# Two-layer streaming encoder: the low part of a pair's two direct factors made by a negation on ACT and an accumulating DMA instead of a subtraction on DVE

## The chip, the cores and the metric

One Trainium2 chip, one core. The metric is the device time of one execution in microseconds, on the core that runs the program; the time before is the median of three runs.

## The reference, cut to what matters

One inference step of a two-layer encoder for 512 prompt frames and 8 x 16 sample frames, so 640 rows of 1024 channels. Layer 0 has an S5 and attention mixer, layer 1 a Mamba-2 mixer. Each layer begins and ends with a gated feed-forward, so there are four of them, and the change lies in these alone:

```python
def swiglu(x, w_gate, w_up, w_down):
    return (jax.nn.silu(x @ w_gate) * (x @ w_up)) @ w_down

x = layer_norm(ALPHA * x + 0.5 * swiglu(x, ffn_w_gate[l, 0], ffn_w_up[l, 0], ffn_w_down[l, 0]),
               ln_g[l, 0], ln_b[l, 0])
```

The weights are float32: gate and up are 1024 x 2816, down is 2816 x 1024. In the kernel the 2816 hidden channels are 22 rows of 128.

## The kernel before

**Arithmetic.** Every float32 factor is split into a high part, cast to the fp32r format, and a low part, the rest. A product is three matmuls: high by high, low by high, high by low. `split` (L99) makes both parts: ACT casts the source into the high part (L100), and DVE subtracts this from the source (L101). The weights arrive by DMA from SP in tiles `raw` of 128 x 1024 (512 KB, four buffers), and the parts are put in tiles `w` (L110: two units of high and low, 128 x 2 x 2 x 512, six buffers) and one single unit `w1` (L107, one buffer).

**Feed-forward.** `ffn` (L226) runs four times, named ffn0, ffn1, ffn2 and ffn3. Rows 0 and 1 and the gate of rows 2 and 3 are computed directly. All other rows go in pairs (`pair`, L400), gate first and up after it, and each is one call of `matrix` (L370) that replaces eight block products of a 2 x 2 by 2 x 2 scheme with seven. A product (L362) is 12 matmuls of 320 columns, so a matrix has 84.

**Operands of a matrix.** `operands` (L339) loads two raw tiles, `r0` with the blocks b11 and b21 and `r1` with b12 and b22. Two of the seven factors, b11 and b21 themselves, are split straight from `r0` into tile u; these are the two direct factors. Then four totals (`total`, L347) are formed in place, over the raw blocks, on DVE: b11 becomes b12 - b11, then b12, b22 and b21 in turn. Between them stand the splits of b22 and of the new b11 (tile v), of the new b12 and b22 (tile w) and of the new b21 (tile o, the single unit). The first total therefore overwrites half of `r0`, from which u has been split. The totals are told to be queued behind the low part of b22 on DVE (`state["lo"]`).

**Order of the products.** TensorE runs the factors in the order 1, 5, 6, 2, 7, 3, 4: u, v, w, u, w, v, o. After product 1 ACT copies the result x into z (L383), since product 6 adds to z; products 5 and 6 are copied aside by ACT (L379). The four quarters of the result leave PSUM by `take`: x (quarter 0,0) after product 2, z (quarter 1,1) after product 7, w (quarter 1,0) after product 3, z (quarter 0,1) after product 4, which goes on adding to z and so waits until the take of (1,1) has been done. For the gate the takes are additions on DVE (L408) and SiLU on ACT (L410), for up they are additions and products on DVE (L416, L418, L420).

**Between the matrices.** Rows are gathered by four. The order is up, gate, up and gate of the next four rows, and then `down` of the earlier four rows; so four matrices stand between two downs, and three before the last down of a feed-forward. In ffn1, ffn2 and ffn3 most downs are `down7` (L463), also with seven products; half of its results go to DVE (L511), half to ACT, which scales them into `ev` (L514), and from there by an accumulating DMA on POOL into `yacc` (L515). In ffn0 and ffn3 side work of the mixers is interleaved.

**Order of instructions.** Each engine runs its own queue in order. A scheduler sets these orders when the program is built, from its own estimates of durations and from the dependencies; semaphore waits follow from the dependencies, on buffers too. So a change of an instruction moves others.

Of the kernel before, what the change touches and what calls it, by code (L numbers as in the profile page):

```python
# [10 lines left out]
F32 = mybir.dt.float32  # L11
# [3 lines left out]
ALU = mybir.AluOpType  # L15
# [22 lines left out]
def kernel(ctx: ExitStack, tc: tile.TileContext, I, O, phases=PHASES):  # L38
    nc = tc.nc
# [31 lines left out]
    def bank_a():  # L71
        return bank(next(state["a"]))
# [26 lines left out]
    def split(hi, lo, src):  # L99
        nc.scalar.copy(hi, src)  # L100
        return nc.vector.tensor_tensor(lo, src, hi.bitcast(F32), op=ALU.subtract)  # L101

    def raw_tile():
        return pools["raw"].tile([128, 1024], F32, name="raw")

    def unit():
        return pools["w1"].tile([128, 2, 512], F32R, name="w1")  # L107

    def two_units():
        return pools["w"].tile([128, 2, 2, 512], F32R, name="w")  # L110

    def split2(w, src):

        return split(w[:, :, 0], w[:, :, 1], src.rearrange("p (j c) -> p j c", j=2))
# [111 lines left out]
    def ffn(i, ph, last, side=None):  # L226
# [4 lines left out]
        with ExitStack() as st:  # L231
# [63 lines left out]
            for r in range(2):  # L295
# [3 lines left out]
                for c in range(2):  # L299
                    p = bank_a()[:, :Q] if r else sums[c]  # L300
# [38 lines left out]
            def operands(src0, src1):  # L339
                r0, r1 = raw_tile(), raw_tile()  # L340
                nc.sync.dma_start(r0, src0)
                nc.sync.dma_start(r1, src1)
                b11, b21, b12, b22 = r0[:, :512], r0[:, 512:], r1[:, :512], r1[:, 512:]
                u, v, w = (two_units() for _ in range(3))
                o = unit()

                def total(o, v, w):  # L347
                    with tc.issue_after(state["lo"]):
                        V.tensor_tensor(o, v, w, op=ALU.subtract)  # L349

                split2(u, r0)
                state["lo"] = split(v[:, 1, 0], v[:, 1, 1], b22).ins
                total(b11, b12, b11)
                split(v[:, 0, 0], v[:, 0, 1], b11)
                total(b12, b22, b12)
                total(b22, b22, b11)
                split2(w, r1)
                total(b21, b21, b22)
                split(o[:, 0], o[:, 1], b21)
                return {1: u[:, 0], 2: u[:, 1], 3: v[:, 1], 4: o, 5: v[:, 0], 6: w[:, 1], 7: w[:, 0]}  # L360
# [39 lines left out]
            def pair(f, before=None):  # L400
# [25 lines left out]
                for n, take in (("w_gate", gate), ("w_up", up)):  # L426
                    if n == "w_gate" and f == 2:
                        tick("gate")
                        continue
                    if n == "w_up" and before is not None:  # L430
                        down(before)
                    with ExitStack() as q:
                        if f == 2:
                            for k in ("acc0", "xc"):
                                if k in state:
                                    q.enter_context(tc.issue_after(state[k]))
                        A = operands(I[n][i, f], I[n][i, f + 1])
                    if n == "w_up":
                        for r in range(2):
                            ht[f + r] = h_tile()  # L440
                    matrix(A, take)
                    if n == "w_up" and seven(f):
                        row_sums(f)
                    tick("gate" if n == "w_gate" else "up")
# [1576 lines left out]
```

## Time and profile before

| what | value |
|---|---|
| median of three runs | 2541.68 us (2533.86 to 2542.25) |
| the profiled execution | 2534.06 us |
| its span in the profile | 2532.4 us |
| mean granted TensorE clock | 0.997 |
| loads of `w_gate`, `w_up`, `w_down` by SP | 88 each, 512 KB |
| data moved by DMA | 324.80 MB |

The page lists busy time by engine, the chain of work that ended last, and groups of instructions by line. PE stands for TensorE's matmuls and PEld for its weight loads, DVE for VectorE, ACT for ScalarE, POOL for GpSimd, SP for SyncE, which issues most DMAs. A row of a window shows its length, then the busy time and count of each engine, the clock, the busy share of the DMA engines and GB/s. A row of the timeline shows start and duration of an instruction, or of several of one kind that follow each other (x2).

### The profile page before, as it was taken

Reading aid. Unit: us, or ns where it says so; the run is one execution under the profiler, and the core shown is the slowest. Engines: PE = TensorE matmul, PEld = TensorE weight load, DVE = VectorE, ACT = ScalarE, POOL = GpSimd, SP = SyncE. Lnnn points to the kernel's source line nnn. Section 1 sums busy time; section 2 is a strip of 40 time slices with the busy share of each in tenths; the row PEclk is TensorE's granted clock in tenths of the full one; section 3 lists DMA queues with packets and bytes.
Section 4 is the critical chain, followed back from the end, with each engine's and each line's share of the span. In section 5 each row is a group of like instructions: output and inputs, shape, how many; then the busy total and the mean of one; then the engine's idle time right before and its main releaser. Section 6 shows DMA issues by size and latency. Waiting matters only on the chain. (4 is left out here: it accounts for less than half of the span.)

```text
span 2532.4 us, 40815 instructions
## 1 busy us (share of the span) xinstructions
PE 2488.3 (98%) x15551; PEld 2282.8 (90%) x15551; DVE 2018.3 (80%) x3505; ACT 1272.1 (50%) x2389; POOL 372.9 (15%) x492
## 2 busy tenths in 40 slices
PE   9999999999999999999999999999999999999998
PEld 8999999878779999999999999999999879999997
DVE  7788777666878888878988887777576789998887
ACT  4443444336744555553455554566565543554542
POOL 0000001210130000013000002311121151112121
PEclk9999999999999999999999999999999999999999
DMA  5332335443221433462144434456464722555563
GB/s 186 109 101 87 107 118 155 144 160 109 84 84 59 116 104 98 113 162 68 59 113 112 121 100 131 150 163 196 151 214 135 244 72 94 158 149 164 154 173 115
DMA packets 179253, 324.80 MB, mean 128 GB/s; under 512 B 21312, under 2 KB 92608, under 8 KB 178544
## 3 DMA queue, kind: packets, MB, share of 16 engines
q1 hardware_dynamic: 165200, 293.83, 36.7%
q0 software_dynamic: 13856, 28.35, 5.7%
q8 instruction: 122, 2.00, 0.3%
q14 instruction: 75, 0.61, 0.1%
HBM read 259.56 MB, written 40.54 MB: 119 GB/s over the span
## 5 line engine op out<-in xcount | busy, mean ns | idle before, releaser
L101 DVE TENSOR_TENSOR w<-raw,w 128x512 fp32r<-128x512 f32 (+2 forms) x721 | 626.4, 890 | 84.0 <-ACT w L100 81.2
L100 ACT CAST w<-raw 128x512 fp32r<-128x512 f32 (+1 forms) x721 | 531.5, 769 | 317.2 <-DVE raw L349 153.2
L366 PE MATMUL bank<-xhi,w 128*128 128x320 f32 x2432 | 540.4, 310 | 2.9 <-DVE s L408 1.9
L146 PE MATMUL bank<-xhi,w 128*128 128x256 f32 (+2 forms) x2272 | 497.6, 311 | 6.7 <-DVE hf L288 1.7
L366 PE MATMUL bank<-T,w 128*128 128x320 f32 x2736 | 428.4, 309 | 3.6 <-ACT bank L383 1.7
L366 PEld LDWEIGHTS bank<-xhi,w 128*128 128x128 f32 x2432 | 406.8, 188 | 8.7 <-DVE s L408 3.1
L366 PEld LDWEIGHTS bank<-T,w 128*128 128x128 f32 x2736 | 407.0, 188 | 6.6 <-ACT bank L383 3.9
L146 PEld LDWEIGHTS bank<-xhi,w 128*128 128x128 f32 x2272 | 376.9, 187 | 16.3 <-issue 3.9
L366 PE MATMUL bank<-xlo,w 128*128 128x320 f32 x1216 | 375.2, 309 | 0.0
L146 PE MATMUL bank<-xlo,w 128*128 128x256 f32 (+2 forms) x1136 | 350.5, 309 | 2.0 <-DVE xlo L211 1.8
L146 PE MATMUL bank<-w,h 128*128 128x512 f32 x1488 | 346.5, 391 | 0.0
L146 PEld LDWEIGHTS bank<-w,h 128*128 128x128 f32 x1488 | 277.1, 188 | 57.5 <-ACT h L100 1.4
L366 PEld LDWEIGHTS bank<-xlo,w 128*128 128x128 f32 x1216 | 228.2, 188 | 0.0
L146 PEld LDWEIGHTS bank<-xlo,w 128*128 128x128 f32 x1136 | 213.6, 188 | 3.3 <-DVE xlo L211 2.1
L349 DVE TENSOR_TENSOR raw<-raw 128x512 f32<-128x512 f32 x304 | 211.5, 696 | 3.4
L515 POOL DMA_DIRECT2D yacc<-ev x84 | 72.6, 888 | 689.4 <-ACT ev L514 610.8
L502 PE MATMUL bank<-w,h 128*128 128x512 f32 x576 | 134.5, 389 | 0.0
L502 PEld LDWEIGHTS bank<-w,h 128*128 128x128 f32 x576 | 108.1, 188 | 22.4
L379 ACT COPY mx<-bank 128x320 f32<-128x320 f32 x152 | 64.6, 425 | 104.4 <-PE bank L366 104.1
L511 DVE SCALAR_TENSOR_TENSOR yacc<-bank,yacc 128x512 f32<-128x512 f32 x84 | 57.8, 688 | 72.0 <-PE bank L502 71.9
L223 DVE SCALAR_TENSOR_TENSOR yacc<-bank,yacc 128x512 f32<-128x512 f32 x120 | 81.8, 686 | 34.1 <-PE bank L146 33.4
L514 ACT ACTIVATE ev<-bank 128x512 f32<-128x512 f32 x84 | 50.2, 597 | 116.2 <-PE bank L502 112.9
(437 smaller groups left out, 3427.6 us busy)
## 6 DMA issues: line engine op xcount, KB each, us to landing
raw<-in_w_gate_dram SPq DMA_DIRECT2D x88, 512.0 KB, 3.6
raw<-in_w_up_dram SPq DMA_DIRECT2D x88, 512.0 KB, 4.1
raw<-in_w_down_dram SPq DMA_DIRECT2D x88, 512.0 KB, 3.6
raw<-in_m_in_dram SPq DMA_DIRECT2D x52, 512.0 KB, 4.4
yacc<-ev POOLq DMA_DIRECT2D x84, 256.0 KB, 4.7
raw<-in_m_out_dram SPq DMA_DIRECT2D x24, 512.0 KB, 4.5
csb<-cs_d SPq DMA_DIRECT2D x20, 512.0 KB, 5.3
h<-in_ssd_h_dram SPq DMA_DIRECT2D x16, 512.0 KB, 6.1
```

What stands on the lines that cost most here:

```text
L100: nc.scalar.copy(hi, src)
L101: return nc.vector.tensor_tensor(lo, src, hi.bitcast(F32), op=ALU.subtract)
L146: state["pe"] = nc.tensor.matmul(ps, a, b, start=(k == 0), stop=(k == n - 1)).ins
L223: state["acc"] = nc.vector.scalar_tensor_tensor(ya, pb, scale, ya, op0=ALU.mult, op1=ALU.add).ins
L349: V.tensor_tensor(o, v, w, op=ALU.subtract)
L366: nc.tensor.matmul(ps, A[p][:, a, k * 128:k * 128 + 128], X[p][b][:, k, :], start=(first and n == 0), stop=(n == 11), skip_group_check=True)
L379: nc.scalar.copy(e[n], ps)
L502: nc.tensor.matmul(ps, a[:, u], b[:, v], start=(first and n == 0), stop=(n == 5), skip_group_check=True)
L511: V.scalar_tensor_tensor(ya, ps, 0.5 / ALPHA, ya, op0=ALU.mult, op1=ALU.add)
L514: nc.scalar.mul(e, ps, 0.5 / ALPHA)
L515: nc.gpsimd.dma_start(yacc[:, t, 512 * j:512 * j + 512], e, accum_op=ALU.add)
```

## The change

In `operands` the one call `split2(u, r0)` is replaced. ACT still casts `r0` into the high parts of u. ACT then multiplies these by -1 into the low parts of u, and POOL issues a DMA that adds `r0` to them; so the low part is again `r0` minus its high part. DVE no longer subtracts there. The DMA reads `r0`, so the first total, which overwrites half of `r0`, has to wait until it has landed; the matmuls with u's low parts wait for it too.

```diff
@@ operands @@
-                split2(u, r0)
+                nc.scalar.copy(u[:, :, 0], r0.rearrange("p (j c) -> p j c", j=2))
+                nc.scalar.mul(u[:, :, 1], u[:, :, 0].bitcast(F32), -1.0)
+                nc.gpsimd.dma_start(u[:, :, 1].bitcast(F32), r0.rearrange("p (j c) -> p j c", j=2),
+                                    accum_op=ALU.add)
                 state["lo"] = split(v[:, 1, 0], v[:, 1, 1], b22).ins
                 total(b11, b12, b11)
```

`operands` is called 76 times. Three lines are added, so later lines of the changed kernel are three higher (L383 is L386 there). The scheduler moves other instructions with it. Three places show how, all from ffn1: the up matrix of rows 6 and 7, whose operands are made while the down of rows 2 to 5 runs, and the gate matrix of rows 8 and 9 after it.

DVE, operands of the up matrix, before; raw_8744 and raw_8745 are `r0` and `r1`, w_8748, w_8749, w_8750 and w1_8751 are u, v, w and o, and w_8887 is u of the gate matrix after it:

```order
L101 TENSOR_TENSOR w_8748<-raw_8744,w_8748 128x2x512 [waits DMAHW2_49,Activation_49]
L101 TENSOR_TENSOR w_8749<-raw_8745,w_8749 128x512 [waits DMAHW3_49,Activation_49]
L349 TENSOR_TENSOR raw_8744<-raw_8745,raw_8744 128x512 [waits DVE_49]
L511 SCALAR_TENSOR_TENSOR yacc_84<-bank_8629,yacc_84 128x512 [waits PE_49]
L349 TENSOR_TENSOR raw_8745<-raw_8745 128x512 [waits DVE_49]
L101 TENSOR_TENSOR w_8749<-raw_8744,w_8749 128x512 [waits Activation_49]
L349 TENSOR_TENSOR raw_8745<-raw_8745,raw_8744 128x512 [waits DVE_49]
L511 SCALAR_TENSOR_TENSOR yacc_84<-bank_8627,yacc_84 128x512 [waits PE_49]
L349 TENSOR_TENSOR raw_8744<-raw_8744,raw_8745 128x512 [waits DVE_49]
L101 TENSOR_TENSOR w_8750<-raw_8745,w_8750 128x2x512 [waits Activation_49]
L101 TENSOR_TENSOR w_8887<-raw_8883,w_8887 128x2x512 [waits DMAHW4_49,Activation_49]
```

DVE, the same place in the changed kernel; raw_8767 and raw_8768 are `r0` and `r1`, w_8772, w_8773 and w1_8774 are v, w and o:

```order
L514 SCALAR_TENSOR_TENSOR yacc_84<-bank_8650,yacc_84 128x512 [waits PE_49]
L101 TENSOR_TENSOR w_8772<-raw_8768,w_8772 128x512 [waits DMAHW3_49,Activation_49]
L514 SCALAR_TENSOR_TENSOR yacc_84<-bank_8652,yacc_84 128x512 [waits DVE_49,PE_49]
L349 TENSOR_TENSOR raw_8767<-raw_8768,raw_8767 128x512 [waits DMAHW2_49,DMASW0_49]
L514 SCALAR_TENSOR_TENSOR yacc_84<-bank_8650,yacc_84 128x512 [waits PE_49]
L349 TENSOR_TENSOR raw_8768<-raw_8768 128x512 [waits DVE_49]
L101 TENSOR_TENSOR w_8772<-raw_8767,w_8772 128x512 [waits Activation_49]
L349 TENSOR_TENSOR raw_8768<-raw_8768,raw_8767 128x512 [waits DVE_49]
L514 SCALAR_TENSOR_TENSOR yacc_84<-bank_8650,yacc_84 128x512 [waits PE_49]
L349 TENSOR_TENSOR raw_8767<-raw_8767,raw_8768 128x512 [waits DVE_49]
L101 TENSOR_TENSOR w_8773<-raw_8768,w_8773 128x2x512 [waits Activation_49]
L101 TENSOR_TENSOR w1_8774<-raw_8767,w1_8774 128x512 [waits Activation_49]
```

Both low parts of u (w_8748 and w_8887) have gone, and the first total of raw_8767 now waits for a DMA of POOL's queue (DMASW), with two results of the down (L511, now L514) and the other totals behind it.

ACT, from v's second high part to the first copies of the up matrix, before; w_8887, w_8888 are u and v of the gate matrix, and L383 is the copy of x into z:

```order
L100 CAST w_8749<-raw_8744 128x512 [waits DVE_49]
L514 ACTIVATE ev_8718<-bank_8626 128x512 [waits DMASW7_49,PE_49,Activation_49]
L100 CAST w_8750<-raw_8745 128x2x512 [waits DVE_49]
L100 CAST w_8887<-raw_8883 128x2x512 [waits DMAHW4_49]
L514 ACTIVATE ev_8734<-bank_8626 128x512 [waits DMASW0_49,PE_49,Activation_49]
L100 CAST w1_8751<-raw_8744 128x512 [waits DVE_49]
L100 CAST w_8888<-raw_8884 128x512 [waits DMAHW5_49,PE_49]
L383 COPY bank_7735<-bank_8768 128x320 [waits PE_49]
L100 CAST w_8888<-raw_8883 128x512 [waits DVE_49]
```

ACT, the same place in the changed kernel; w_8911 and w_8912 are u and v of the gate matrix, L386 is the copy into z and L352 the negation:

```order
L100 CAST w_8772<-raw_8767 128x512 [waits DVE_49]
L517 ACTIVATE ev_8757<-bank_8649 128x512 [waits DMASW7_49,PE_49]
L100 CAST w_8773<-raw_8768 128x2x512 [waits DVE_49]
L351 CAST w_8911<-raw_8907 128x2x512 [waits DMAHW4_49]
L100 CAST w1_8774<-raw_8767 128x512 [waits DVE_49]
L386 COPY bank_7754<-bank_8792 128x320 [waits PE_49]
L352 ACTIVATE w_8911<-w_8911 128x2x512 [waits Activation_49]
L382 COPY mx_8819<-bank_8793 128x320 [waits PE_49]
L100 CAST w_8912<-raw_8908 128x512 [waits DMAHW5_49]
L382 COPY mx_8833<-bank_7754 128x320 [waits PE_49]
L100 CAST w_8912<-raw_8907 128x512 [waits DVE_49]
```

The negation for the gate matrix now stands behind the copy into z of the up matrix, which waits for PE, and so the DMA that follows it is issued later than that; v's first high part moves behind that copy and the next one as well.

DVE, operands of the gate matrix and the first takes of the up matrix (L416, L418), before; raw_8883 and raw_8884 are the gate's `r0` and `r1`:

```order
L349 TENSOR_TENSOR raw_8883<-raw_8884,raw_8883 128x512 [waits DVE_49]
L349 TENSOR_TENSOR raw_8884<-raw_8884 128x512 [waits DVE_49]
L101 TENSOR_TENSOR w_8888<-raw_8883,w_8888 128x512 [waits Activation_49]
L349 TENSOR_TENSOR raw_8884<-raw_8884,raw_8883 128x512 [waits DVE_49]
L349 TENSOR_TENSOR raw_8883<-raw_8883,raw_8884 128x512 [waits DVE_49]
L101 TENSOR_TENSOR w_8889<-raw_8884,w_8889 128x2x512 [waits Activation_49]
L416 TENSOR_TENSOR hf_8823<-bank_8768,s_8514 128x320 [waits PE_49]
L101 TENSOR_TENSOR w_9008<-raw_9004,w_9008 128x2x512 [waits DMAHW6_49,Activation_49]
L418 TENSOR_TENSOR hf_8837<-bank_7735,mx_8795 128x320 [waits PE_49]
```

DVE, the same place in the changed kernel, where the takes are L419 and L421 and the gate's tiles raw_8907 and raw_8908:

```order
L101 TENSOR_TENSOR w_8912<-raw_8908,w_8912 128x512 [waits DMAHW5_49,Activation_49]
L419 TENSOR_TENSOR hf_8847<-bank_8792,s_8537 128x320 [waits PE_49]
L349 TENSOR_TENSOR raw_8907<-raw_8908,raw_8907 128x512 [waits DMAHW4_49,DMASW4_49]
L349 TENSOR_TENSOR raw_8908<-raw_8908 128x512 [waits DVE_49]
L421 TENSOR_TENSOR hf_8861<-bank_7754,mx_8819 128x320 [waits PE_49]
L101 TENSOR_TENSOR w_8912<-raw_8907,w_8912 128x512 [waits Activation_49]
L349 TENSOR_TENSOR raw_8908<-raw_8908,raw_8907 128x512 [waits DVE_49]
L421 TENSOR_TENSOR hf_8861<-bank_8793,mx_8833 128x320 [waits PE_49]
```

Before, all four totals and w's low part stood ahead of the take of (0,0). Now the first total, with its wait for the DMA, stands between that take and the take of (1,1), and w's low part has moved behind all takes of the up matrix.

## Prediction before the run

> **What bounds the kernel now.** I read the page's busy times first, then the end of the chain, a table of windows over one stretch of the feed-forward, and the timeline of that stretch.
>
> ```profile
> span 2532.4 us, 40815 instructions
> PE 2488.3 (98%) x15551; PEld 2282.8 (90%) x15551; DVE 2018.3 (80%) x3505; ACT 1272.1 (50%) x2389; POOL 372.9 (15%) x492
> ```
>
> ```profile
> 2501.66 0.47 PE bank L1491 x2
> ```
>
> PE is idle for 2532.4 - 2488.3 = 44.1 us, and the chain leaves PE at 2502.1, so 30.3 of these are the tail of the last layer norm. Only some 14 us are left between the matmuls. No edit off PE can win more.
>
> The second feed-forward (ffn1), from the end of its first seven-product down, stage by stage (four matrices, then the next down):
>
> ```profile
> core 0: us, PE busy (x) PEld busy (x) DVE busy (x) ACT busy (x) POOL busy (x), PEclk, DMA share, GB/s
> 881.40:893.70 12.30, 12.30 (x85) 12.27 (x84) 11.50 (x18) 6.10 (x11) 0.85 (x1) 1.00 0.63 166
> 893.70:906.00 12.30, 12.30 (x86) 12.30 (x85) 11.84 (x22) 7.87 (x16) 0.00 (x0) 1.00 0.28 88
> 906.00:918.30 12.30, 12.30 (x86) 12.30 (x85) 8.61 (x12) 6.84 (x10) 0.00 (x0) 1.00 0.26 85
> 918.30:930.60 12.30, 12.30 (x86) 12.30 (x85) 12.03 (x22) 6.92 (x14) 0.00 (x0) 1.00 0.15 44
> 930.60:955.00 24.40, 24.40 (x110) 20.23 (x109) 17.16 (x24) 11.92 (x17) 5.14 (x6) 1.00 0.62 139
> ```
>
> PE never stops, at full clock, and a matrix lasts 12.3 us. DVE is busy for 11.5 to 12.0 of 12.3 us in three of four: DVE just keeps up, and a DVE that has to wait there soon makes PE wait.
>
> **What is removed and added.** There are 304 totals (L349) at four per call, so `operands` runs 76 times.
>
> ```profile
> L101 DVE TENSOR_TENSOR w<-raw,w 128x1024 fp32r<-128x1024 f32 x248 | 301.4, 1228 | 28.5 <-ACT w L100 27.8
> L100 ACT CAST w<-raw 128x1024 fp32r<-128x1024 f32 x248 | 255.3, 1050 | 137.8 <-DVE raw L349 55.4 <-PE bank L366 26.4 <-PE bank L146 25.4
> L349 DVE TENSOR_TENSOR raw<-raw 128x512 f32<-128x512 f32 x304 | 211.5, 696 | 3.4
> L515 POOL DMA_DIRECT2D yacc<-ev x84 | 72.6, 888 | 689.4 <-ACT ev L514 610.8 <-DMA yacc<-ev 56.1 <-ACT w L100 18.4
> ```
>
> DVE loses 76 x 1.23 = 93 us of work. Since PE is idle in none of these windows, that alone is worth nothing. ACT gets 76 negations; none is in the trace, and I take the cast of the same shape, 1.05 us: 80 us more on an engine that is half idle, free as busy time, but 1.05 us in a chain. POOL gets 76 issues of about 0.9 us, harmless by themselves.
>
> The price is a wait. The first total writes b11 over half of `r0`, which the DMA now reads. Before, it followed the subtraction on DVE's own queue; now it waits until the transfer has landed. Queued behind it on DVE are the other totals, the low parts of v, w and o, and the takes that empty PE's banks; behind the casts that need those totals stand, on ACT, the copy of `r0` for the next matrix and the copies into z that PE needs.
>
> **How long the add takes.** An accumulating DMA of 512 KB is not in the trace. The nearest rows are the 256 KB ones from `ev` to `yacc`: first all 84 from issue to landing, then queue 0 in the window 864 to 886, where it carries seven of them and nothing else, then plain 512 KB loads on the same queue.
>
> ```profile
> DMA to landing us min/median/max: 3.3/4.7/6.6
> ```
>
> ```profile
> q0 software_dynamic: 1004, 1.83, 47.5%
> ```
>
> ```profile
> T<-in_ln_gb_dram POOLq DMA_DIRECT2D x8, 512.0 KB, 5.4
> ```
>
> Seven took 47.5% of 22 us on all engines, so 1.5 us each. Another 256 KB adds 1.5 us: 4.7 + 1.5 = 6.2 us, which I take, being nearest to the row of the same operation and above the plain load. The ends are 3.3 (the shortest, if size cost nothing) and 9.4 (twice the median); 4.8 and 8.1 come from the shortest and longest plus 1.5.
>
> **The walk through one stretch.** Times are from E = 881.43, PE's first matmul after the down. The first rows are DVE and ACT, the last PE.
>
> ```profile
> 872.79 1.57 ACT L100 CAST w<-raw 128x1024 fp32r<-128x1024 f32 x2
> 875.81 0.69 DVE L349 TENSOR_TENSOR raw<-raw 128x512 f32<-128x512 f32 x1
> 878.22 0.69 DVE L349 TENSOR_TENSOR raw<-raw 128x512 f32<-128x512 f32 x1
> 878.94 2.00 ACT L100 CAST w<-raw 128x1024 fp32r<-128x1024 f32 x2 [0.74 <-DVE raw L349]
> ...
> 881.33 1.13 ACT L100 CAST w<-raw 128x512 fp32r<-128x512 f32 x2
> ...
> 883.39 0.41 ACT L383 COPY bank<-bank 128x320 f32<-128x320 f32 x1 [0.93 <-PE bank L366]
> ```
>
> ```profile
> 890.99 0.48 DVE L418 TENSOR_TENSOR hf<-bank,mx 128x320 f32<-128x320 f32 x1
> ```
>
> ```profile
> 881.43 0.46 PE L366 MATMUL bank<-xhi,w 128*128 128x320 f32 x2
> ...
> 893.74 0.45 PE L366 MATMUL bank<-xhi,w 128*128 128x320 f32 x2
> ```
>
> A matrix is 12.31 us, seven products of 1.76. Product 6, third, adds to z and needs the copy into z by 3.5; the last needs the take of (1,1) by 10.55.
>
> *Up of rows 6 and 7.* The copy of `r0` and the high part of b22 end at -7.1, the negation at -6.0, the add lands at +0.2. Before, the first total began at 875.81, -5.6: 5.8 us later now. Two totals, a take, v's low part and another total run to 3.2 at 0.6 each. ACT then casts w (4.3), copies the next `r0` (5.3) and casts o (5.9), and only then copies z (6.3). Before, that copy ended at 2.4, so a cover of 1.1 us is gone and PE waits 6.3 - 3.5 = 2.8.
>
> *The next add.* Its negation now stands behind the z copy: 6.3 to 7.4, landed at 13.6. Two totals run to 14.9 and the take of (1,1) to 15.4; the last product could start at 10.55 + 2.8 = 13.4, so PE waits 2.0 more, and this matrix ends at 17.2. Before, that take began at 890.99, 9.6.
>
> *Gate of rows 8 and 9.* w's low part now stands behind eleven rows of takes, sums and low parts and ends at 23.2; its product needs it at 20.9: 2.3. The next negation ends at 22.4, the add lands at 28.6, three DVE rows and the take run to 30.9, needed at 30.1: 0.8. End 32.7.
>
> *Up of rows 8 and 9.* z copied 0.3 late; negation ends 36.1, add lands 42.3, six DVE rows and the take run to 46.1, needed at 43.6: 2.5. End 47.9, where PE needs 36.9. The fourth matrix holds no add and catches nothing up.
>
> So such a stretch loses 2.8 + 2.0 + 2.3 + 0.8 + 0.3 + 2.5 = 10.7, say 11 us. A check: from one add to the next run the add 6.2, three totals 2.1, cast of w 1.05, copy 1.05, cast of o 0.6 and negation 1.05, 12.1 us without the copies and SiLUs between them (0.4 to 2 us), against 12.3 for PE. The circle is just longer than a matrix. Walked again with 5.0 us the stretch loses 6.2: some 4 us of loss per us of landing.
>
> **The sum.** A feed-forward has five stretches: three like this, 33; the last without its fourth matrix, about 8; the first, where the walk finds three waits of 2.4, 0.2 and 2.8, 5.5. That is 46.5, and 4 x 46.5 = 186 us. I price ffn0 and ffn3 alike, though the side work in them moves rows. On the profiled execution's own time, 2534.06 us: 2720. The median shown, 2541.68, is 7.6 above it: **2728 us**.
>
> **Rivals.**
>
> *The add is hidden, and it is no slower.* If size cost nothing and each add landed like the shortest row, in 3.3 us, the first total would come at -2.7, the z copy in time, and each take before its due. It decides at about 3.8 us: below, the first landing in a stretch still leaves the copies their slack. The gate's late low part alone remains (DVE order, not landing), at most 1 us in four stretches per feed-forward, 16 us, of which DVE's 1.2 us less per matrix gives some back in ffn3, where PE is short by 0.2 to 1.9 us per 50:
>
> ```profile
> 2150.00:2200.00 50.00, 48.10 (x320) 46.72 (x319) 47.72 (x74) 28.02 (x49) 5.21 (x4) 1.00 0.46 150
> ...
> 2350.00:2400.00 50.00, 49.84 (x279) 45.10 (x278) 43.70 (x64) 24.95 (x40) 11.10 (x11) 1.00 0.60 162
> ```
>
> Some +7 remains: 2549, within 0.5%. Against it: only the shortest of 84 is so fast, at half the size. Chance 0.08. The Trainium skill (DMA: Bandwidth & Descriptors, "Anatomy of one DMA") fits a DMA from GpSimd with 2.0 us plus bytes at 436 GB/s, which for 512 KB gives an estimate of 3.2 us and so this case. By that fit the 256 KB rows should take 2.6 us; the trace shows 4.7, so I do not follow it.
>
> *Worse landing.* Each matrix loads 1 MB of weights, and 12.3 us now also carry 3.0 us of add on the same engines; the add's issue stands behind POOL's own waits (L515 idles 689.4 us in all). In ffn3 the DMA share is already 0.46 to 0.60. With 8.1 us a stretch loses 11 + 1.9 x 4 = 18.6, and all of it 186 x 18.6 / 11 = 315: 2857. For it: more traffic than in any window here. Against it: the measured 4.7 already includes neighbours in the same queue. Chance 0.17.
>
> **How the numbers follow.** The forecast, with landings from 4.6 to 7.3, has 0.75. At 7.3 the sum is 186 x 15.4 / 11 = 260, 2802; at 4.6 it is 186 x 4.6 / 11 = 78, 2620. I put the range at 2615 to 2810; left out are the hidden add and most of the worse landing. About 0.5%, 12.7 us, is what a measurement of this kernel can tell from no change. Slower takes the forecast, the worse landing: 0.92; same 0.06; faster 0.02, since 14 us of idle PE is all there is.
>
> **What would show it.** In the changed profile the first total should be DVE's costliest wait, on the add from POOL, some 3 to 6 us each time; the add should take about 6 us to land; PE should be busy for near 2488 us still, but idle some 230, behind ACT's copy into z, DVE's takes and DVE's low part of w; the four windows should read 13 to 17 us instead of 12.3, and the downs still 24. The forecast is wrong if adds land under 4 us, if DVE reaches the first total late anyway, or if PE idles on something else, such as weights that load late.

## The result, and the profile after

The changed kernel takes **2786.28 us** (median of five runs, 2784.65 to 2792.93) against 2541.58 us for the kernel before (also five runs, 2533.86 to 2542.25), a ratio of 1.098 with a 95% interval of 1.096 to 1.100. It is slower, inside the range of 2615 to 2810, and 58 us above the predicted 2728. The profiled execution took 2792.93 us.

The page of the changed kernel:

```profile
span 2791.2 us, 40959 instructions
PE 2573.0 (92%) x15551; PEld 2342.9 (84%) x15551; DVE 1940.7 (70%) x3429; ACT 1338.3 (48%) x2465; POOL 462.3 (17%) x568
```

The span grew by 2791.2 - 2532.4 = 258.8 us. PE's idle time went from 44.1 to 218.2 us, so 174 us of it is waiting. The other 85 us is PE's busy time, 2573.0 against 2488.3, for the same 15551 matmuls. DVE lost 78 us of work and ACT gained 66; neither number is in the span.

**The wait.** From the waits of the changed kernel (engine, tile and line, what released it: us in total, times, longest):

```profile
DVE raw L349 <- DMA w<-raw: 302.6, 69, 7.7
PE bank L369 <- DVE hf L421: 60.6, 27, 4.9
PE bank L369 <- DVE s L411: 52.1, 14, 5.7
PE bank L505 <- DVE yacc L514: 34.2, 12, 6.1
PE bank L369 <- ACT mx L382: 12.4, 9, 2.8
PE bank L369 <- DVE w L101: 3.1, 6, 1.3
```

The first total now waits for the add in 69 of 76 calls, 4.4 us each; before, all 304 totals together had 3.4 us of idle time ahead of them. PE in turn waits for what is queued behind that total on DVE: the takes of the up matrix (hf), of the gate (s), and the results of the down (yacc). The add itself, from issue to landing:

```profile
DMA to landing us min/median/max: 5.0/6.6/9.8
```

**One stretch.** The same stretch as in the prediction (ffn1, behind the first seven-product down), matrix by matrix, in windows of the changed kernel:

```profile
933.75:951.10 17.35, 14.67 (x89) 14.40 (x88) 10.12 (x18) 8.63 (x13) 1.35 (x2) 0.90 0.44 107
951.10:968.30 17.20, 13.48 (x82) 13.02 (x81) 11.09 (x19) 8.43 (x16) 1.20 (x1) 0.90 0.38 92
968.30:985.20 16.90, 14.43 (x88) 14.16 (x87) 9.37 (x14) 7.52 (x12) 1.22 (x1) 0.90 0.48 120
985.20:997.60 12.40, 12.40 (x86) 12.32 (x85) 11.71 (x21) 7.91 (x15) 0.00 (x0) 1.00 0.15 51
```

Three matrices with an add last about 17 us instead of 12.3, the fourth, without one, 12.4. DVE is now busy for 9 to 11 of 17 us: it waits. And the clock, the column behind POOL, has fallen to 0.90 in just these three windows. The timeline shows both causes: ACT's negation (L352), POOL's issue (L353) and DVE's first total (L349), then PE:

```profile
936.46 0.42 ACT L386 COPY bank<-bank 128x320 f32<-128x320 f32 x1
936.82 1.05 ACT L352 ACTIVATE w<-w 128x1024 fp32r<-128x1024 f32 x1
...
938.16 1.20 POOL L353 DMA_DIRECT2D w<-raw  x1 [4.26 <-ACT w L352]
...
945.12 1.42 DVE L349 TENSOR_TENSOR raw<-raw 128x512 f32<-128x512 f32 x2 [3.79 <-DMA w<-raw]
...
962.50 1.42 DVE L349 TENSOR_TENSOR raw<-raw 128x512 f32<-128x512 f32 x2 [5.65 <-DMA w<-raw]
...
977.14 1.42 DVE L349 TENSOR_TENSOR raw<-raw 128x512 f32<-128x512 f32 x2 [5.23 <-DMA w<-raw]
```

```profile
932.25 1.66 PE L505 MATMUL bank<-w,h 128*128 128x512 f32 x6 [1.69 <-DVE yacc L514]
...
942.40 1.92 PE L369 MATMUL bank<-T,w 128*128 128x320 f32 x12
946.99 0.56 PE L369 MATMUL bank<-xhi,w 128*128 128x320 f32 x2 [2.68 <-DVE hf L421]
...
947.56 0.74 PE L369 MATMUL bank<-xhi,w 128*128 128x320 f32 x2
...
951.27 0.46 PE L369 MATMUL bank<-xhi,w 128*128 128x320 f32 x2
...
965.02 0.90 PE L369 MATMUL bank<-xhi,w 128*128 128x320 f32 x2 [3.72 <-DVE s L411]
...
981.40 0.73 PE L369 MATMUL bank<-xhi,w 128*128 128x320 f32 x2 [2.48 <-DVE hf L421]
```

The add issued at 938.16 has landed by 945.1, 7 us later; DVE stands for 3.79 us, PE for 2.68. Behind each such gap a pair of matmuls takes 0.74 us instead of 0.46 for 3 to 4 us. In a window of that time and in one behind it:

```profile
947.50:951.10 3.60, 3.60 (x16) 3.60 (x15) 3.27 (x8) 2.93 (x4) 0.00 (x0) 0.53 0.00 0
951.30:952.10 0.80, 0.80 (x7) 0.80 (x7) 0.80 (x3) 0.70 (x2) 0.00 (x0) 1.00 0.00 0
```

PE is never idle there, and the granted clock is 0.53. The three matrices last 51.45 us, 36.93 at full pace; 8.88 us of the difference are the three gaps, the other 5.6 us are in the slower matmuls behind them.

### The profile page after: what moved, and what is told of

It reads as the page before. It is cut to its first block, busy times and chain, and to the rows that moved or that the text cites. A ratio compares the mean times of both kernels' runs of the same rounds, so it can differ in the third digit from the quotient of the medians.

```text
span 2791.2 us, 40959 instructions
## 1 busy us (share of the span) xinstructions
PE 2573.0 (92%) x15551; PEld 2342.9 (84%) x15551; DVE 1940.7 (70%) x3429; ACT 1338.3 (48%) x2465; POOL 462.3 (17%) x568
## 5 line engine op out<-in xcount | busy, mean ns | idle before, releaser
L100 ACT CAST w<-raw 128x512 fp32r<-128x512 f32 (+1 forms) x645 | 458.4, 735 | 561.3 <-DVE raw L349 438.7
L369 PE MATMUL bank<-xhi,w 128*128 128x320 f32 x2432 | 586.1, 329 | 125.3 <-DVE hf L421 60.6
L101 DVE TENSOR_TENSOR w<-raw,w 128x512 fp32r<-128x512 f32 (+1 forms) x645 | 543.3, 861 | 123.5 <-ACT w L100 121.7
L369 PEld LDWEIGHTS bank<-xhi,w 128*128 128x128 f32 x2432 | 440.0, 204 | 144.7 <-DVE hf L421 68.8
L349 DVE TENSOR_TENSOR raw<-raw 128x512 f32<-128x512 f32 x304 | 210.4, 692 | 305.8 <-DMA w<-raw 302.6
L146 PEld LDWEIGHTS bank<-xhi,w 128*128 128x128 f32 x2272 | 380.3, 189 | 19.7 <-issue 4.9
L369 PE MATMUL bank<-xlo,w 128*128 128x320 f32 x1216 | 394.4, 324 | 0.0
L146 PE MATMUL bank<-w,h 128*128 128x512 f32 x1488 | 348.0, 392 | 1.5 <-ACT h L100 1.5
L369 PEld LDWEIGHTS bank<-xlo,w 128*128 128x128 f32 x1216 | 246.3, 203 | 0.4
L353 POOL DMA_DIRECT2D w<-raw x76 | 94.7, 1247 | 806.9 <-ACT w L352 529.9
L146 PEld LDWEIGHTS bank<-xlo,w 128*128 128x128 f32 x1136 | 215.3, 190 | 3.3 <-DVE xlo L211 2.0
L505 PE MATMUL bank<-w,h 128*128 128x512 f32 x576 | 144.0, 403 | 36.1 <-DVE yacc L514 34.2
L505 PEld LDWEIGHTS bank<-w,h 128*128 128x128 f32 x576 | 109.8, 193 | 64.4 <-DVE yacc L514 38.6
L514 DVE SCALAR_TENSOR_TENSOR yacc<-bank,yacc 128x512 f32<-128x512 f32 x84 | 57.9, 689 | 77.0 <-PE bank L505 76.9
L146 PE MATMUL bank<-w,og 128*128 128x512 f32 x432 | 103.8, 395 | 0.9 <-DVE og L101 0.8
```

The lines of the kernel that those rows point to most:

```text
L146: state["pe"] = nc.tensor.matmul(ps, a, b, start=(k == 0), stop=(k == n - 1)).ins
L353: nc.gpsimd.dma_start(u[:, :, 1].bitcast(F32), r0.rearrange("p (j c) -> p j c", j=2), accum_op=ALU.add)
L369: nc.tensor.matmul(ps, A[p][:, a, k * 128:k * 128 + 128], X[p][b][:, k, :], start=(first and n == 0), stop=(n == 11), skip_group_check=True)
L505: nc.tensor.matmul(ps, a[:, u], b[:, v], start=(first and n == 0), stop=(n == 5), skip_group_check=True)
L514: V.scalar_tensor_tensor(ya, ps, 0.5 / ALPHA, ya, op0=ALU.mult, op1=ALU.add)
```

## The experiments

Three theories. **A**: the price is the first total's wait for the landed add, on the circle copy, negation, add, totals, casts, next copy; the longer matmuls follow from PE's gaps. **B**: the adds' traffic, or POOL's issues, slow the kernel by themselves. **C**: ACT's negation, in front of copies that PE needs, is the cost. Ratios are to the kernel before, run on the same chip beside each.

**1. No total over r0 (e1b).** The adds stay; in three of four feed-forwards nothing waits for them but the matmuls.

```diff
-                total(b11, b12, b11)
-                split(v[:, 0, 0], v[:, 0, 1], b11)
+                t11, t21 = (wk.tile([128, 512], F32, name=n, bufs=1) if ph != "ffn3" else b
+                            for n, b in (("t11", b11), ("t21", b21)))
+                total(t11, b12, b11)
+                split(v[:, 0, 0], v[:, 0, 1], t11)
                 total(b12, b22, b12)
-                total(b22, b22, b11)
+                total(b22, b22, t11)
                 split2(w, r1)
-                total(b21, b21, b22)
-                split(o[:, 0], o[:, 1], b21)
+                total(t21, b21, b22)
+                split(o[:, 0], o[:, 1], t21)
```

> The changed kernel, but in ffn0, ffn1 and ffn2 the totals that would overwrite r0 write into two tiles of their own, so that no total waits for the add; ffn3, where no room is left, stays as changed. All 76 adds and negations remain. Theory A (the cost is the wait of the first total for the landed add, on the circle of copy, negation, add, totals, casts, and the half-rate matmuls that follow PE's gaps): the losses of ffn0 to ffn2 (42 + 64 + 67 us of the 245) go and ffn3's 78 stay: 2615 to 2640 us, PE busy falls by some 55 us from 2573, and the first total's wait on the add is there 19 times instead of 69. Theory B (the traffic of the adds or POOL's issues slow the kernel by themselves): 2740 to 2790. Theory C (ACT's negation, in front of the copies that PE needs, is the cost): 2720 to 2790.

Measured: 2612.41 us, ratio 1.029 (1.027 to 1.030), just under the interval that A gave. POOL's loads of layer-norm rows (L171) mark the phases: the first of T stands at the end of ffn0, the first of h ahead of ffn3, the last of T behind it. Before, changed, and this kernel:

```profile
L171 POOL DMA_DIRECT2D T<-in_ln_gb_dram x8: 538/550/598, 414.6 to 2489.2; - x8
...
L171 POOL DMA_DIRECT2D h<-in_ln_gb_dram x2: 543/602/660, 1992.0 to 1992.7; - x2
```

```profile
L171 POOL DMA_DIRECT2D T<-in_ln_gb_dram x8: 546/570/598, 456.6 to 2748.0; - x8
...
L171 POOL DMA_DIRECT2D h<-in_ln_gb_dram x2: 548/602/655, 2172.9 to 2173.6; - x2
```

```profile
L171 POOL DMA_DIRECT2D T<-in_ln_gb_dram x8: 546/570/598, 412.9 to 2565.4; - x8
...
L171 POOL DMA_DIRECT2D h<-in_ln_gb_dram x2: 551/603/655, 1993.3 to 1994.0; - x2
```

Up to ffn3 this kernel is as fast as the one before (1993.3 against 1992.0; the changed one is at 2172.9), with all its adds and negations. From there to the last load it takes 572.1 us, the changed kernel 575.1, the one before 497.2. So where no total waits, the loss is gone, and where it still waits, in ffn3, nearly all of it has stayed (75 of 78 us).

**2. The first total alone moved (e1).** The fourth total still writes over b21:

```diff
-                total(b11, b12, b11)
-                split(v[:, 0, 0], v[:, 0, 1], b11)
+                t11 = wk.tile([128, 512], F32, name="t11", bufs=1) if ph != "ffn3" else b11
+                total(t11, b12, b11)
+                split(v[:, 0, 0], v[:, 0, 1], t11)
                 total(b12, b22, b12)
-                total(b22, b22, b11)
+                total(b22, b22, t11)
```

> The changed kernel, but in ffn0, ffn1 and ffn2 the first total alone writes into a tile of its own; the fourth total (b21) still overwrites half of r0 and waits for the add. ffn3 stays as changed. The kernel with both totals moved took 2612. Theory A, with the wait at the fourth total: the three links ahead of it (two more totals of 0.7 and the low part of v) and the cast of w run while the add is under way, so some 3 of the 6.6 us of landing are covered; by my slope the losses of ffn0 to ffn2 fall from 173 to 0 to 60: 2612 to 2670 us. If it is the whole row behind whichever total waits that counts: 2740 or more.

Measured: 2653.49 us, ratio 1.045 (1.044 to 1.047), in A's interval. Its wait:

```profile
DVE raw L349 <- DMA w<-raw: 195.0, 57, 8.0
```

Fewer and shorter waits, but not none: the fourth total comes some 3 us behind the first (945.1 and 948.4 in the changed kernel's stretch), and that covers a part of the landing only.

**3. The add on DVE (e2).**

```diff
-                nc.gpsimd.dma_start(u[:, :, 1].bitcast(F32), r0.rearrange("p (j c) -> p j c", j=2),
-                                    accum_op=ALU.add)
+                V.tensor_tensor(u[:, :, 1], r0.rearrange("p (j c) -> p j c", j=2), u[:, :, 1].bitcast(F32), op=ALU.add)
```

> The changed kernel with the accumulating DMA replaced by an addition on DVE of the same data; the negation on ACT stays. Theory A: no total waits for a DMA, DVE has its old load again, ACT carries 80 us more; one link of 1.05 us (the negation) is added ahead of DVE's row: 2540 to 2580 us, PE busy back near 2490. Theory B: near 2541 as well, since the DMA is gone. Theory C: the negations alone cost most of it, so 2650 to 2790.

Measured: 2540.48 us, ratio 1.000 (0.999 to 1.001).

```profile
PE 2493.0 (98%) x15551; PEld 2285.9 (90%) x15551; DVE 2026.0 (80%) x3505; ACT 1336.7 (53%) x2465; POOL 376.2 (15%) x492
```

ACT carries all its negations (1336.7 us busy) and the time is that of the kernel before. C falls: the negation is free both as busy time and as one more link, once DVE takes the add up at once.

**4. An add beside the old subtraction, from r0 (e3), and elsewhere (e4).** Both are the kernel before with a transfer whose result is unused:

```diff
+                if ph != "ffn3":
+                    nc.gpsimd.dma_start(junk, r0, accum_op=ALU.add)
```

```diff
+                if ph != "ffn3":
+                    nc.gpsimd.dma_start(junk, zero, accum_op=ALU.add)
```

> The kernel before, with DVE's subtraction, and beside it in ffn0, ffn1 and ffn2 an accumulating DMA of 512 KB from r0 into a tile that nobody reads (extra work, 57 adds). The first total must wait for it here too, but it can be issued as soon as r0 has landed from memory, without copy and negation ahead of it. Theory A: the wait is there but the circle is shorter by copy, negation and the wait for ACT's turn; it lands ahead of DVE's first total in most matrices: 2541 to 2610 us. If a reader of r0 by DMA always costs what it did: 2541 + 173 = 2714. Theory B (traffic): 2680 to 2720.

> The kernel before, and beside it in ffn0, ffn1 and ffn2 an accumulating DMA of 512 KB from a tile of zeros into a tile that nobody reads (extra work, 57 adds): the same traffic and POOL issues, with no wait for anyone but POOL. Theory A and C: 2541 to 2556 us, nothing that can be measured. Theory B: the traffic costs as it did, 2680 to 2720.

Measured: 2542.02 us from r0, ratio 1.001 (1.000 to 1.002), and 2551.15 us elsewhere, ratio 1.004 (1.003 to 1.006). The first: what POOL waited for before the issue, and the first total's row:

```profile
POOL junk L357 <- DMA raw<-in_w_up_dram: 575.5, 28, 39.1
```

```profile
L353 DVE TENSOR_TENSOR raw<-raw 128x512 f32<-128x512 f32 x304 | 211.7, 696 | 11.8 <-DMA junk<-raw 8.3
```

Here too a DMA reads r0 and the first total must wait until it has landed. But POOL issues it when the weights arrive, not behind a copy and a negation, and so it is over when DVE gets there: 8.3 us of waiting in all instead of 302.6. So a DMA that reads r0 costs nothing as such; it costs when it starts late. The second kernel's 11.6 us lie inside A's range, but nothing that could be measured was expected. Part of it is at the start, where nothing holds the adds back and they run in a bunch (DMA share 0.89 against 0.56 before, PE busy 50.95 of 60 us against 55.66):

```profile
0.00:60.00 60.00, 50.95 (x315) 49.03 (x316) 40.12 (x83) 28.89 (x54) 11.85 (x18) 0.97 0.89 257
```

```profile
0.00:60.00 60.00, 55.66 (x347) 53.05 (x348) 47.07 (x96) 30.12 (x56) 3.81 (x9) 1.00 0.56 196
```

So in these three feed-forwards B is worth 0 to 12 us. The changed kernel had lost 181 us by the end of them (2172.9 against 1992.0 by the marks of experiment 1).

**5. Two adds of 256 KB, b11's half first (e5).**

```diff
-                nc.gpsimd.dma_start(u[:, :, 1].bitcast(F32), r0.rearrange("p (j c) -> p j c", j=2),
-                                    accum_op=ALU.add)
+                for j in range(2):
+                    nc.gpsimd.dma_start(u[:, j, 1].bitcast(F32), r0[:, 512 * j:512 * j + 512], accum_op=ALU.add)
```

> The changed kernel with the add issued as two DMAs of 256 KB, that of b11 first; the first total waits for the first alone. POOL has 76 issues more. Theory A: the first total comes 1 to 2 us earlier (the shorter issue and half the bytes; the nearest row, of 256 KB into yacc, lands in 4.7 instead of 6.6), the fourth total waits for the second: some 4 us of loss per us of landing and stretch, 20 stretches: 80 to 160 us less, 2630 to 2710. Theory B (traffic): no less than 2786, since the bytes are the same and the issues doubled.

Measured: 2662.22 us, ratio 1.049 (1.048 to 1.051). The wait and the landing:

```profile
DVE raw L349 <- DMA w<-raw: 176.7, 74, 8.0
```

```profile
DMA to landing us min/median/max: 3.3/4.6/9.5
```

The same bytes in more issues take off half of the loss. The landing is 2.0 us shorter (4.6 against 6.6), PE's idle time 87 us less (131.3 against 218.2): 44 us per us of landing. The prediction's slope, 4 us per stretch and 16.9 stretches' worth, was 68. The split also lets the first total wait for b11's half alone, so that this is one comparison and not the price of the landing by itself.

**6. Half by DVE, half by DMA (e6).** b11's low part is subtracted on DVE, so that the first total waits for nothing; b21's comes from a negation and an add of 256 KB.

```diff
-                nc.scalar.mul(u[:, :, 1], u[:, :, 0].bitcast(F32), -1.0)
-                nc.gpsimd.dma_start(u[:, :, 1].bitcast(F32), r0.rearrange("p (j c) -> p j c", j=2),
-                                    accum_op=ALU.add)
+                nc.scalar.mul(u[:, 1, 1], u[:, 1, 0].bitcast(F32), -1.0)
+                V.tensor_tensor(u[:, 0, 1], b11, u[:, 0, 0].bitcast(F32), op=ALU.subtract)
+                nc.gpsimd.dma_start(u[:, 1, 1].bitcast(F32), b21, accum_op=ALU.add)
```

> The changed kernel with b11's low part subtracted on DVE again (half the length, 128 x 512) and only b21's low part made by negation (128 x 512 on ACT) and a 256 KB add. The first total waits for nothing new, the fourth for the add. DVE keeps half of the gain of 93 us. Theory A: the fourth total comes some 4 us after u's casts, the add lands in 4.7 plus 0.6 for the negation: little waiting is left, 2541 to 2600. If a single accumulating DMA in each circle costs in proportion to its bytes: 2541 + 245 / 2 = 2663.

Measured: 2564.41 us, ratio 1.011 (1.009 to 1.013). The fourth total's wait:

```profile
DVE raw L349 <- DMA w<-raw: 56.0, 25, 5.0
```

Its adds land in 4.0 us (median), most of them ahead of the fourth total. The cost is not in proportion to the bytes: half of them cost a tenth, since the total that waits for them comes later.

**7. PE's gaps filled (e7).** 60 unused products stand where PE waits, to see whether the gaps slow the matmuls.

```diff
+                if fill:
+                    product(bank("b")[:, :Q], A, 1, True)
...
-                    matrix(A, take)
+                    matrix(A, take, n == "w_up" or f % 4 == 0)
```

> The changed kernel with 12 more matmuls (product 1 once more, into a bank that nobody reads) between products 3 and 4 of every up matrix and of the gate that follows a down: 60 times 1.76 us at full clock, 106 us of unused work, just where PE waits for the take of (1,1). Question: the 85 us by which the same 15551 matmuls became longer. Theory A with the clock: gaps of 2.5 us and more let PE's matmuls fall to half rate for some us; the fill shortens the gaps before product 4 below that, so PE's busy time beyond the fill falls by 30 to 60 us, idle time by 60 to 100, and the whole comes to 2740 to 2800 in spite of 106 us more work. If the matmuls are longer for another reason (operands read beside more DMA traffic): busy time is 2573 + 106 = 2679, idle 120 to 160, 2800 to 2840.

Measured: 2799.07 us, ratio 1.104 (1.101 to 1.106).

```profile
PE 2640.2 (94%) x16271; PEld 2418.2 (87%) x16271; DVE 1946.4 (70%) x3429; ACT 1341.9 (48%) x2465; POOL 460.2 (16%) x568
```

720 more matmuls, 106 us at full clock, cost 13 us of time. PE's busy time rose by 67 us only, so the other matmuls became some 39 us shorter in sum; idle time fell by 63 us to 155.2; the mean clock rose from 0.969 to 0.984. By the other reading busy time would have been 2679. So nearly half of the 85 us goes when these gaps are filled.

The clock records in the traces say what most of the 85 us are. Half the clock was granted for 173 us of the changed kernel's span, for 89 with the fill and for 17 before the change. PE was at work in 150, 78 and 10 us of these, and half of that, 75, 39 and 5 us, is what the slower clock cost. So 70 of the 85 us are the clock's, and its fall from 75 to 39 is nearly the whole of what the fill took off the other matmuls. The remaining 15 us stay open. That the whole did not get faster fits the circle: it, and not PE, seems to set the pace.

**8. A second reader behind the add (e8), and one more link (e10).** Two tests of the slope, and both missed it.

```diff
+                if ph != "ffn3":
+                    nc.gpsimd.dma_start(junk[:, :512], b11, accum_op=ALU.add)
```

> The changed kernel, and in ffn0, ffn1 and ffn2 behind each add a second accumulating DMA that adds the b11 half of r0 (256 KB) to a tile that nobody reads (57 unused transfers); the first total waits for both. It makes the wait longer and nothing else. Theory A, by the slope of the prediction (4 us per stretch and us of landing, 15 stretches in these three feed-forwards): the second lands 1.5 to 2.5 us behind the first (1.5 us of queue time for 256 KB, or that and 0.9 us of issue): 90 to 150 us more, 2875 to 2935. Theory B (traffic): half of the added bytes again costs half of 173, about 87 us: 2870. The two differ in where: by A the first total's wait on DVE grows by 1.5 us or more each; by B PE waits for something else.

Measured: 2795.63 us, ratio 1.101 (1.099 to 1.103), 9 us more than the changed kernel, whose interval (1.096 to 1.100) overlaps with this one.

```profile
POOL junk L360 <- DMA raw<-in_w_up_dram: 367.4, 27, 33.8
```

The second transfer needs only r0, so it was issued when the weights arrived, often ahead of the first; the scheduler did not keep the order of the code. It lengthened no wait (the totals waited 304.0 us in all, 250.8 of them put down to the add, against 302.6), and what it measured instead is B: 57 more transfers of 256 KB cost 9 us at most by the medians.

```diff
-                nc.scalar.mul(u[:, :, 1], u[:, :, 0].bitcast(F32), -1.0)
+                nc.scalar.copy(u[:, :, 1], u[:, :, 0].bitcast(F32))
+                nc.scalar.mul(u[:, :, 1], u[:, :, 1].bitcast(F32), -1.0)
```

> The changed kernel with one more link in the circle: ACT copies the high parts of u into the low parts and negates them there, two operations of 1.05 us instead of one, ahead of each of the 76 adds; the values are the same. It adds 80 us to ACT, which is half idle, and 1.05 us to the circle. Theory A, by the slope of the prediction (4 us per stretch and us, so 68 us for all stretches): 71 us more idle time of PE, and with half as much again for the slower matmuls behind its gaps 106 us: 2855 to 2895 us. If the wait for the add were set by the weights' arrival or by POOL, the link would vanish in it: 2786 to 2800. Busy time alone (all 80 us of ACT laid on top) would give 2866 with PE's busy time unchanged at 2573.

Measured: 2812.69 us, ratio 1.107 (1.106 to 1.109), 26 us more instead of 70 to 106.

```profile
DVE raw L349 <- DMA w<-raw: 244.9, 69, 6.9
PE bank L370 <- DMA w<-raw: 91.1, 47, 5.6
```

```profile
DMA to landing us min/median/max: 5.0/5.6/10.0
```

The adds landed in 5.6 instead of 6.6 us, which takes back what the link adds, and PE now waits for the add itself, in u's low part, 91.1 us in all, where it had waited mostly for the takes. PE's busy time is 13 us longer than in the changed kernel (2585.8), though half the clock was granted for 117 us only. So the slope per link was not isolated; why the adds landed sooner and why PE was busy for longer stay open. Laying 80 us of ACT on top is ruled out as well.

**9. The add from memory (e9).** The raw weights are fetched a second time, so that no DMA reads r0 in any feed-forward.

```diff
-                nc.gpsimd.dma_start(u[:, :, 1].bitcast(F32), r0.rearrange("p (j c) -> p j c", j=2),
+                nc.gpsimd.dma_start(u[:, :, 1], src0.rearrange("p (j c) -> p j c", j=2).bitcast(F32R),
```

> The changed kernel, but the accumulating DMA reads the raw weights from memory once more (76 times 512 KB, 39 MB more traffic from memory) instead of from r0; nothing reads r0 by DMA, so that no total waits, in ffn3 too. The matmuls with u's low part still wait for the add. Theory A: no wait of a total is left; DVE has 93 us less to do, which is worth nothing: 2535 to 2560 us. Theory B (traffic): 2600 or more, above all in ffn3, where the DMA engines are busy 46 to 60% before the change. If PE's wait for u's low part matters: 1 to 3 us in the first matrix after each down, 18 times: 2560 to 2595.

Measured: 2550.35 us, ratio 1.004 (1.003 to 1.005).

```profile
PE 2493.0 (98%) x15551; PEld 2288.6 (90%) x15551; DVE 1940.5 (76%) x3429; ACT 1340.2 (53%) x2465; POOL 451.6 (18%) x568
```

```profile
L351 ACT CAST w<-raw 128x1024 fp32r<-128x1024 f32 x76 | 79.6, 1047 | 30.6 <-DMA raw<-in_w_up_dram 17.0 <-PE bank L369 13.3
```

```profile
DMA to landing us min/median/max: 5.4/5.7/11.4
```

All 76 negations and adds are there, each lands in 5.7 us (median), 40 MB more come from memory, and 96% of the loss is gone. 10 us are left. In the profiled execution most of what is left lies in ffn3, where B looked for it: by the marks of L171 ffn3 takes 511.7 us here, 497.2 before and 575.1 in the changed kernel. ACT's cast of r0 now stands 17.0 us for weights that arrive later. Neither is shown to be the cause of the 10 us. DVE has 78 us less to do here than before the change and the kernel is no faster for it.

No version beats the kernel before: only some 14 us of PE's idle time were there to win.

## Why the prediction was right, and where it was off

*What bounds the kernel.* Right. With DVE's work removed and no total waiting (experiment 9) the time is 0.4% above that of before, and with ACT's added and DVE's restored (experiment 3) the same as before. So neither 78 us off DVE nor 66 on ACT is worth anything here.

*The wait and its size.* Right. The landing was taken at 6.2 us, by the 256 KB rows and another 1.5; it measured 6.6 (5.0 to 9.8). The first total is DVE's costliest wait, 4.4 us each.

*The walk.* Right in sum, not in its places. For the stretch it gave 10.7 us of idle PE; the trace has 8.9 within the matrices and 1.69 at the end of the down ahead of them, 10.6. But the first wait, 2.8 us for the copy into z, was not there: that copy stands at 936.46, 2.7 us behind PE's first matmul, in time. PE had been held before that, in the down, because two of the down's results queue on DVE behind the waiting total. The prediction named them as queued there and did not price them; they cost 34.2 us in all. The low part of w, 2.3 us late by the walk, cost 3.1 us in the whole kernel; the takes cost more instead, 3.72 us in the gate against 0.8. The downs did not stay at 24 us either: the next one takes 26.6 (997.1 to 1023.7), for the same reason as the one ahead of the stretch.

*The sum of idle time.* 186 us foreseen, 174 measured. The mechanism, a circle a little longer than a matrix, is right; that the sum comes so near is in part luck, since two waits of the walk, 2.8 and 2.3 us, did not come and others were larger by as much.

*PE's busy time.* Here it failed. "PE should be busy for near 2488 us still" was wrong by 85 us, and so the sum, which priced gaps at their length only, came out too small. The step was to take a gap's price as its length and the matmuls behind it as unchanged; 70 of the 85 us are the clock's (experiment 7). The matmuls of xhi and w:

```profile
L366 PE MATMUL bank<-xhi,w 128*128 128x320 f32 x2432 | 540.4, 310 | 2.9 <-DVE s L408 1.9 <-ACT mx L379 0.7 <-DVE hf L418 0.4
```

```profile
L369 PE MATMUL bank<-xhi,w 128*128 128x320 f32 x2432 | 586.1, 329 | 125.3 <-DVE hf L421 60.6 <-DVE s L411 52.1 <-ACT mx L382 12.4
```

The upper row is of before. Product 4, which stands behind the takes, is among these, and they grew from 310 to 329 ns, 46 us in all. Those of xlo and w, in the same products, grew from 309 to 324 ns, 19 us; a part of the down (L505) grew by 9.5 us; those of T and w grew by 2 ns only. 174 + 85 = 259 is the whole growth of the span.

*The slope.* Given as 4 us of loss per stretch and us of landing, 68 us for all stretches. Experiment 5 shows 44 us of idle time per us, or 62 of the whole time. The two tests made for it failed, so it rests on that one comparison.

*The rivals.* The hidden add needed landings under 3.8 us; the shortest of 76 took 5.0. The fit of the Trainium skill (DMA: Bandwidth & Descriptors, "Anatomy of one DMA") gave an estimate of 3.2 us; the trace has none so short, and the measurement decides. Worse landing by traffic (8.1 us) did not come: 6.6, and more traffic by itself cost 0 to 12 us (experiments 4, 8 and 9). The measured time lies between the forecast and this rival, but for another reason, PE's longer busy time. The range was made for landings of 4.6 to 7.3 us and had no place for the slower clock, so that it holds the measured time is in part luck.

*ffn0 and ffn3 priced alike.* Not so: by the marks of L171 ffn0 lost 42 us and ffn3 78, the slower matmuls included.

## What to carry to other kernels

An operation that goes from an engine to a DMA takes the DMA's landing into every later write over its source; look first for who overwrites that source in place, and either give the DMA another source, as in experiment 9, or start it early, as the unused add from r0 in experiment 4 was. Where the engine that loses the work does not set the end, the gain is nothing, and the new wait is the whole effect. And a gap on PE is not priced at its length alone: look in the windows at the clock behind it.

## What the runs showed of the hardware that was not expected

The clock can fall behind short gaps. After PE's gaps of 2.48, 2.68 and 3.72 us the granted clock was about 0.5 for 3 to 4 us, after one of 1.69 us it was not, and after another of 2.65 us neither. The windows behind these last two, with the clock 1.00:

```profile
932.25:935.85 3.60, 3.60 (x21) 3.33 (x22) 3.60 (x6) 2.31 (x3) 0.86 (x1) 1.00 0.71 122
447.25:450.85 3.60, 3.60 (x24) 3.60 (x25) 3.44 (x6) 2.82 (x6) 0.00 (x0) 1.00 0.41 131
```

So the gap's length alone does not decide. Of the gaps in this trace, half clock came during or within 1.5 us of the end of all 21 of 3 us and more, of 13 of the 23 between 2 and 3 us, and of 2 of the 15 between 1.5 and 2 us. It cost about 1.9 us for each of the three gaps of the stretch, and 70 us beside 174 us of idle time over the kernel. The Trainium skill (TensorE: Matmul & The Clock Gate, "Part 1: The HAM clock gate") describes a half rate after an idle window of about 3.4 us; here gaps below that were enough. No run here shows why.

The same 512 KB were dearer to issue in more and shorter pieces. The add into the contiguous tile (experiment 4, from r0), then the one into u, whose low parts are two separate runs in each partition; behind the bar POOL's busy time and the mean ns of one:

```profile
L357 POOL DMA_DIRECT2D junk<-raw x57 | 50.8, 892 | 717.6 <-DMA raw<-in_w_up_dram 575.5 <-DMA raw<-in_w_gate_dram 100.3 <-DMA junk<-raw 26.3
```

```profile
L353 POOL DMA_DIRECT2D w<-raw x76 | 94.7, 1247 | 806.9 <-ACT w L352 529.9 <-PE bank L369 69.2 <-DVE T L101 39.3
```

0.89 us against 1.25. 256 KB in one run in each partition took 0.89 before the change (yacc, L515), as much as 512 KB in as many runs. The landings, 5.5 and 6.6 us, can't be put down to the pieces: the same add into u landed in 5.6 us in the longer circle and in 6.1 in experiment 1.
